# A hybrid HGRN2 / RWKV-7 layer on one core: level 0 from the forget gate, norms and sums in written order, output operands split behind the last in-projection column, one more step at sums and states

## The chip, the cores and the metric

The kernel runs on one core of one Trainium2 chip. The metric is the device time of one launch in microseconds, the median of three runs. The engines are named as in the profile: PE (TensorE, with PEld for its weight loads), DVE (VectorE), ACT (ScalarE), POOL (GpSimd, here mostly a queue that issues DMAs) and SP (SyncE, the other such queue).

## The reference

One decoder layer on x of 1 × 2048 × 1024, all in float32. In short (the recurrences are written out step by step; the kernel computes them by chunks of 64 tokens):

```python
h = _rmsnorm(x, norm1_w[l])
proj = h @ w_in[l]                       # 1024 -> 3840
hg_p, rw_p = proj[..., :HG_COLS], proj[..., HG_COLS:]

# HGRN2: 4 heads of 128
f = lb + (1.0 - lb) * sigmoid(f_raw)
q = silu(q_raw) * 128 ** -0.5
k = 1.0 - f
S = f_t * S + k_t v_t^T;  o_t = S^T q_t
o_hg = rms(o) * norm_w * silu(g_raw)

# RWKV-7: 8 heads of 64, token shift, low-rank decay / rate / gate
S = S * w_t + (S a_t) b_t^T + v_t k_t^T;  y_t = S r_t
o_rw = (groupnorm(y) * ln_w + ln_b + bonus) * g

x = x + concatenate([o_hg, o_rw], axis=-1) @ w_out[l]
x = x + _conv_ffn(_rmsnorm(x, norm2_w[l]), w_up[l], conv_w[l], conv_b[l], w_down[l])
```

and a final RMSNorm.

## The kernel before

The work falls into two phases. Phase 1, up to about 1314 us of the span, computes the in-projection, both recurrences, the output projection of three of the four token blocks and the second norm. Phase 2 computes the rest of the output projection and the ConvFFN with a Strassen-like split into seven products, for which sums of quarters of the operands are formed ahead (`four_sums`, L238). The diff touches phase 1 only.

Products of float32 operands are made of three matmuls on operands that are split into a high and a low part (`mm3`, L267 to L272): high × high, low × high, high × low. A split is a cast on ACT and a subtraction on DVE (`split_to`, L247 and L248, `split`, L254 and L255). All activations are issued through `act` (L122), which loads an activation table (L118) whenever the wanted function lies in another set than the last one.

Phase 1 interleaves three generators in program order:

- `dense` walks through a list of jobs. For each of the four blocks of 512 tokens there are 30 in-projection columns of 128 (job "P": eight k steps of three matmuls, each yielding 648 by its own count of ns). Columns are computed from the operands hh and hl, the split and normed x of the block, and are evicted from the PSUM banks `pj` (two of them) by `ev_q`, `ev_f`, `ev_v`, `ev_g`, `ev_rkv`, `ev_lora` and `ev_gd`. Among the columns stand extra jobs: loads of the next block's rows (`load4`), their norms (`norm4`, with `rstd`, L128, whose Square writes the tile nsq), the transposes into hh and hl ("T", `turn`, L443) and the transposes of the second norm ("N", L264). At the start of block 2 stands the output projection of block 0 ("O", `out_block`), at the start of block 3 that of block 1, and at the end that of block 2, whose operands are split by `o_take`.
- `rw_stream` runs eight `rw_super`, one for each block and half of the RWKV heads.
- `hg_stream` runs sixteen `hg_unit`, one for each block and HGRN2 head.

One turn of the main loop takes one step of `rw_stream`, one step of `hg_stream`, each up to its next `yield`, and then steps of `dense` until 2000 ns by its counts are used up (`TICK`, `fill`). So a `yield` more in a recurrence puts some 2000 ns of dense work by that count between the code ahead of it and the code behind it. Tile, the framework, then orders each engine's instructions: an instruction may move ahead of earlier written ones of its engine when its inputs are expected sooner. `tc.keep_in_program_order(i)` keeps an instruction behind all those that are written ahead of it on its engine. Data waits are made by semaphores.

The places that the change and the prediction name:

- L847: the matmuls of `rw_super` that multiply with the inverse; their results lie in the two banks `rw` and are copied by ACT into UV (x4) and M (x3). L867 is the first product behind it (tile xp, in one of the same two banks), L881 the products of M, with the additions L884 and L887 on DVE. L905 and L910 are the chain over the eight chunks, XH the state (L912).
- `hg_unit`: k = 1 − f (L947, tile hk, one buffer), the scaled operands hX of levels 0 to 6 (`scaled`, L971), the output product (L1064, L1065), the sum of squares (tile osq in hk's buffer, split into part, L1083 and L1084), the last products (L1076, L1077) and the store to oT.
- `out_block`: 32 weight tiles woraw (L395, loaded through POOL into the four buffers of the tag wraw, split at L254) and, for blocks 0 and 1, the operands oraw (L388, loaded through SP into two buffers of the tag sg and split into hh and hl during the first pass).

Of the kernel before, what the change touches and what calls it, by code (L numbers as in the profile page):

```python
# [7 lines left out]
F32 = mybir.dt.float32  # L8
# [59 lines left out]
def tile_layer(ctx, tc, consts, x, norm1_w, w_in, hg_lb_logits, hg_norm_w, rw_shift_mu, rw_w0, rw_w2,  # L68
# [56 lines left out]
            tab["uses"].append(i_)  # L125
        return i_

    def rstd(pool, xt, name, sqt="nsq", sqb=1):  # L128

        sq = pool.tile([P, D], BF16, tag=sqt, name="nsq", bufs=sqb)  # L130
        st = pool.tile([P, 2], F32, tag="nst", name=name, bufs=8)
        act(sq, xt, AF.Square, accum_out=st[:, 0:1])
        act(st[:, 1:2], st[:, 0:1], AF.Ln, bias=eps6, scale=1.0 / D)
        act(st[:, 1:2], st[:, 1:2], AF.Exp, scale=-0.5)
        return st[:, 1:2]
# [101 lines left out]

    def four_sums(b11, b12, b21, b22):  # L238

        V.tensor_sub(b11, b12, b11)  # L240
        V.tensor_sub(b12, b22, b12)
        V.tensor_sub(b22, b22, b11)
        V.tensor_sub(b21, b21, b22)
        return b11, b22, b12, b21
# [29 lines left out]
    def phase1(c1):  # L274
# [104 lines left out]
        def out_block(nb, oh=None, ol=None, then=None):  # L379


            for i2 in range(2):
                for dh in range(2):
                    accs = [bank("pj") for _ in range(2)]
                    for k in range(KD):
                        if i2 == 0 and dh == 0 and oh is None:
                            raw = stg("sg", "oraw", 2)
                            dma(raw, oT[nb][k * P:(k + 1) * P, :])  # L388
                            split_to(hh[:, k, :], hl[:, k, :], raw)
                        if i2 == 1 and dh == 0 and oh is not None:  # L390
                            raw = stg("sg", "oraw", 2)[:, 0:256]
                            dma(raw, oT[nb][k * P:(k + 1) * P, 256:512])
                            split_to(hh[:, k, 256:512], hl[:, k, 256:512], raw)
                        raw = wp.tile([P, 512], F32, tag="wraw", name="woraw", bufs=4)
                        wload(raw, w_out[0, k * P:(k + 1) * P, dh * 512:dh * 512 + 512])  # L395
                        wh, wl = split(wp, raw, [P, 512], "w", 4)
                        if k == KD - 2:
                            inputs = dh == 0 and (i2 == 0) == (oh is None)
                            xh = [wp.tile([P, BLK], F32, tag="wraw", name="xh", bufs=4) if inputs else
                                  stg("sg", "xh", 2) for _ in range(2)]  # L400
                            for q in range(2):
                                t0 = nb * BLK + (i2 * 2 + q) * P
                                dma(xh[q], x[0, t0:t0 + P, dh * 512:dh * 512 + 512])
                        for q in range(2):
                            is_ = slice((i2 * 2 + q) * P, (i2 * 2 + q + 1) * P)
                            lhs = ((hh[:, k, is_], hl[:, k, is_]) if oh is None or i2 == 1 else
                                   (oh[k // 4][:, k % 4, is_], ol[k // 4][:, k % 4, is_]))
                            mm3(accs[q], lhs, (wh, wl), k == 0, k == KD - 1)
                            if i2 == 1 and dh == 1 and q == 1:
                                next_block(then, k)  # L410
                            yield 680
                    for q in range(2):
                        V.tensor_add(xh[q], accs[q], xh[q])
                        r0 = (i2 * 2 + q) * P
                        (nc.gpsimd.dma_start if nb == NBLK - 2 and i2 and dh else dma)(
                            x1d[nb][r0:r0 + P, dh * 512:dh * 512 + 512], xh[q])
# [10 lines left out]
        def norm4(key):  # L427
            def f():
                for i in range(4):
                    t_ = rows[key][:, i, :]  # L430
                    V.tensor_scalar_mul(t_, t_, rstd(wp, t_, "nst", "wraw", 4))
            return f

        def four_tiles(t_):
# [12 lines left out]
        def split_h(nb, k):  # L447
# [3 lines left out]
            act(h4, src, AF.Copy, scale=w)  # L451
            V.scalar_tensor_tensor(l4, src, w, h4.bitcast(F32), ALU.mult, ALU.subtract)

        def next_block(nb, k):

            if nb is not None and nb < NBLK:
                for k_ in ([k - 2] if 2 <= k < KD - 1 else [k - 2, k - 1, k] if k == KD - 1 else []):
                    split_h(nb, k_)

        def sum_load(m):  # L460

# [12 lines left out]
        def o_take(m):  # L474

            def f():
                if m == 0:
                    t_ = xp_.tile([P, 2, 2, 4, 256], F32R, tag="xt", name="ohl", bufs=1)
                    rows["O"] = [[t_[:, c, i] for i in range(2)] for c in range(2)]
                t_ = wp.tile([P, 2, 256], F32, tag="wraw", name="oraw", bufs=4)  # L480
                dma(t_, oT[2][2 * m * P:2 * (m + 1) * P, 0:256].rearrange("(k p) t -> p k t", p=P))
                ks = slice(2 * (m % 2), 2 * (m % 2) + 2)
                split_to(rows["O"][0][m // 2][:, ks, :], rows["O"][1][m // 2][:, ks, :], t_)
            return f

        def to_h(k, tp, w):
# [29 lines left out]
        def dense():  # L516
# [64 lines left out]
            for n, jb in enumerate(jobs):  # L581
                if jb[0] == "E":
                    jb[1]()
                    continue
                if jb[0] == "A":
                    if jb[1] == 0:
                        banks = spread()
                        ahead = transposed(four_tiles(rows[0]), "n1", lambda: next(banks), to_h)
                    continue
                if jb[0] == "T":  # L590
                    yield from turn(jb[1])
                    continue
# [12 lines left out]
                while not cond():  # L605
                    yield None
                load(i)
                ws = loaded.pop(i)
                if i == 0:
                    next(ahead)  # L610
                    next(ahead)
                    constants()
                load(i + 1)
                i += 1
                acc = bank("pj")
                then = jobs[n + 1][1] if jobs[n + 1][0] == "A" else None
                for k in range(KD):
                    wh, wl = ws[k // 4]
                    next(ahead, None)
                    mm3(acc, (wh[:, k % 4, :], wl[:, k % 4, :]), (hh[:, k, :], hl[:, k, :]), k == 0, k == KD - 1)  # L620
                    if k == KD - 1:
                        ev(acc)
                        if fin is not None:
                            fin()
                    next_block(then, k)
                    yield 648

        def last_dma(nb):
# [18 lines left out]
        def rw_super(nb, s_):  # L647
# [208 lines left out]
            for e in range(2):  # L856
                r0, c0 = er0(e), col0(1, e)
                act(M[r0:r0 + 64, 0, 1, :, :, 0:64], quv[1][c0:c0 + 64, :, :, 0:64], AF.Copy)
            yield
            XH = tile_("XH", [2, 9, 64], "XH")  # L860
            V.tensor_copy(XH[:, :, 0, :], Xc[:, 2 * s_:2 * s_ + 2, :])
            xp = bank2()
# [81 lines left out]
        def hg_unit(nb, j):  # L944
# [15 lines left out]
            def scaled(l):  # L960
# [4 lines left out]
                V.tensor_mul(vw(X)[:, :, 1, :], vw(q)[:, :, 1, :], vw(Pf)[:, :, 1, :])  # L965
                n_ = BLK // (2 * m)
                if l == 0:
                    act(vw(X)[:, :, 0, :], vw(k)[:, :, 0, :], AF.Copy)
                    act(vw(Sf)[:, :, 0, :], vw(Pf)[:, :, 1, :], AF.Copy)
                else:  # L970
                    V.tensor_mul(vw(X)[:, :, 0, :], vw(k)[:, :, 0, :], vw(Sf)[:, :, 0, :])  # L971
                    V.tensor_mul(vw(Sf)[:, :, 0, :], vw(Sf)[:, :, 0, :],
                                 vw(Pf)[:, :, 1, m - 1:m].broadcast_to([P, n_, m]))
# [106 lines left out]
            yield  # L1080

# [543 lines left out]
```

## Time and profile before

| | us |
|---|---|
| runs | 2646.72, 2646.23, 2655.82 (median 2646.72) |
| the profiled execution: its time | 2645.42 |
| its span, first to last instruction | 2643.6 |
| PE busy over the span | 2547.0 (96%) |
| ACT busy over the span | 1372.7 (52%) |
| DVE busy over the span | 1963.7 (74%) |
| mean granted TensorE clock | 0.994 |

The profile is that of one execution. PE is busy for nearly the whole span, and the chain of waits lies for 70% on PE; a busy PE is not one at its peak, since matmuls are pipelined. What a change in phase 1 is worth is therefore read from PE's idle time there, from what ends it, and from the stretches with a lower granted clock.

### The profile page before, as it was taken

Reading aid. Unit: us, or ns where it says so; the run is one execution under the profiler, and the core shown is the slowest. Engines: PE = TensorE matmul, PEld = TensorE weight load, DVE = VectorE, ACT = ScalarE, POOL = GpSimd, SP = SyncE. Lnnn points to the kernel's source line nnn. Section 1 sums busy time; section 2 is a strip of 40 time slices with the busy share of each in tenths; the row PEclk is TensorE's granted clock in tenths of the full one; section 3 lists DMA queues with packets and bytes.
Section 4 is the critical chain, followed back from the end, with each engine's and each line's share of the span. In section 5 each row is a group of like instructions: output and inputs, shape, how many; then the busy total and the mean of one; then the engine's idle time right before and its main releaser. Section 6 shows DMA issues by size and latency. Waiting matters only on the chain.

```text
span 2643.6 us, 51054 instructions
## 1 busy us (share of the span) xinstructions
PE 2547.0 (96%) x19467; PEld 2046.8 (77%) x19467; DVE 1963.7 (74%) x3744; ACT 1372.7 (52%) x2258; POOL 382.1 (14%) x686
## 2 busy tenths in 40 slices
PE   7999999999999999899899999999999999999998
PEld 5877777777777767777678888887888887888887
DVE  4868677676576765777678789988988887766556
ACT  5555444555545555344466654556554544545444
POOL 6433222212222122232100000000000000000000
PEclk9999999999999999999999999999999999999999
DMA  8846463555655565845583467747763553998655
GB/s 304 239 147 195 152 168 116 143 159 205 190 173 138 174 212 179 261 151 150 181 287 124 136 221 257 240 154 232 245 203 129 171 171 128 334 321 283 200 191 187
DMA packets 380298, 518.98 MB, mean 196 GB/s; under 512 B 114463, under 2 KB 211093, under 8 KB 380053
## 3 DMA queue, kind: packets, MB, share of 16 engines
q1 hardware_dynamic: 325521, 337.38, 40.1%
q0 software_dynamic: 54464, 178.32, 20.9%
q8 instruction: 153, 2.51, 0.4%
q14 instruction: 92, 0.75, 0.1%
q10 hardware_dynamic: 68, 0.02, 0.0%
HBM read 372.99 MB, written 134.22 MB: 192 GB/s over the span
## 4 chain that ended last, share of the span: by engine, by line
PE 70%; DVE 11%; ACT 8%; DMA 7%; issue 3%; POOL 0%; SPq 0%; DVEq 0%; ACTq 0%; POOLq 0%
PE pj L270 7%; PE pj L271 7%; PE pj L272 6%; PE ua L270 5%; PE ua L272 5%; PE ua L271 5%; PE da L271 3%; PE da L272 3%; PE da L270 3%; PE ud L271 2%; PE ud L270 2%; PE ud L272 2%; PE db L272 2%; PE db L271 2%; PE db L270 2%
## 5 line engine op out<-in xcount | busy, mean ns | idle before, releaser
L270 PE MATMUL pj<-hh,wh 128*128 128x512 f32 x960 | 391.6, 408 | 6.1 <-ACT rkv L122 4.0
L271 PE MATMUL pj<-hl,wh 128*128 128x512 f32 x960 | 377.4, 393 | 0.0
L272 PE MATMUL pj<-hh,wl 128*128 128x512 f32 x960 | 377.4, 393 | 0.0
L270 PE MATMUL ua<-Bh,uwh 128*128 128x512 f32 x704 | 276.4, 393 | 3.5 <-ACT m L122 2.2
L272 PE MATMUL ua<-Bh,uwl 128*128 128x512 f32 x704 | 274.3, 390 | 0.0
L271 PE MATMUL ua<-Bl,uwh 128*128 128x512 f32 x704 | 274.1, 389 | 0.0
L270 PEld LDWEIGHTS pj<-hh,wh 128*128 128x128 f32 x960 | 180.9, 189 | 54.5 <-issue 7.0
L272 PEld LDWEIGHTS pj<-hh,wl 128*128 128x128 f32 x960 | 180.8, 188 | 39.4 <-DMA wl<-Win171l 0.3
L271 PEld LDWEIGHTS pj<-hl,wh 128*128 128x128 f32 x960 | 181.0, 189 | 35.0 <-DVE hl L488 0.5
L254 ACT CAST uwh<-uraw 128x512 fp32r<-128x512 f32 x220 | 134.3, 617 | 135.0 <-PE ua L271 55.7
L255 DVE TENSOR_TENSOR dal<-draw,dah 128x512 fp32r<-128x512 f32 x138 | 95.2, 690 | 108.3 <-ACT dah L254 105.7
L255 DVE TENSOR_TENSOR uwl<-uraw,uwh 128x512 fp32r<-128x512 f32 x220 | 147.1, 684 | 34.3 <-ACT uwh L254 34.3
L254 ACT CAST dah<-draw 128x512 fp32r<-128x512 f32 x138 | 85.8, 621 | 160.0 <-PE da L271 75.5
L270 PEld LDWEIGHTS ua<-Bh,uwh 128*128 128x128 f32 x704 | 132.2, 188 | 33.9 <-ACT m L122 5.6
L272 PEld LDWEIGHTS ua<-Bh,uwl 128*128 128x128 f32 x704 | 132.2, 188 | 28.1 <-DVE uwl L255 0.4
L271 PEld LDWEIGHTS ua<-Bl,uwh 128*128 128x128 f32 x704 | 132.3, 188 | 26.7
L270 PE MATMUL ud<-Bh,uwh 128*128 128x512 f32 x352 | 138.0, 392 | 0.0
L1495 POOL DMA_DIRECT2D gd<-y x2 | 1.1, 542 | 943.1 <-DVE y L1493 943.1
L272 PE MATMUL ud<-Bh,uwl 128*128 128x512 f32 x352 | 137.1, 390 | 0.0
L271 PE MATMUL ud<-Bl,uwh 128*128 128x512 f32 x352 | 137.0, 389 | 0.0
L271 PE MATMUL da<-dbl,dah 128*128 128x512 f32 x332 | 129.4, 390 | 0.2 <-DVE dbl L255 0.2
L272 PE MATMUL da<-dbh,dal 128*128 128x512 f32 x332 | 129.2, 389 | 0.0
(582 smaller groups left out, 6203.0 us busy)
## 6 DMA issues: line engine op xcount, KB each, us to landing
uraw<-in_w_up_dram SPq DMA_DIRECT2D x176, 256.0 KB, 3.2
woraw<-in_w_out_dram POOLq DMA_DIRECT2D x96, 256.0 KB, 3.6
br<-gd SPq DMA_DIRECT2D x88, 256.0 KB, 4.3
draw<-Sg SPq DMA_DIRECT2D x88, 256.0 KB, 3.0
draw<-Tw SPq DMA_DIRECT2D x88, 256.0 KB, 3.9
gd<-y SPq DMA_DIRECT2D x86, 256.0 KB, 3.0
Sg<-br SPq DMA_DIRECT2D x72, 256.0 KB, 2.2
xt<-x1d SPq DMA_DIRECT2D x32, 512.0 KB, 6.5
```

Of the source, the lines that this page charges most:

```text
L254: S.copy(hi, src)
L255: V.tensor_sub(lo, src, hi.bitcast(F32))
L270: TE.matmul(acc, lh, rh, start=first, stop=False, skip_group_check=skip)
L271: TE.matmul(acc, lh, rl, start=False, stop=False, skip_group_check=skip)
L272: TE.matmul(acc, ll, rh, start=False, stop=last, skip_group_check=skip)
L1495: (dma if end is None else nc.gpsimd.dma_start)(gd_[2 * h + b][fb * P:(fb + 1) * P, :], ys[0][:, b * BLK:(b + 1) * BLK])
```

## The change

It has seven parts. (1) The Square of the norms in `norm4` is kept in program order. (2) So is the first subtraction of `four_sums`, on which the other three depend. (3) The operands oraw of O 0 and O 1 are loaded and split by a new function `next_out` behind the k steps of the last in-projection column ahead of the block (operand k−2 behind step k), into buffers of the tag wraw, where the weights wraw and woraw lie too; that column now waits, in program order, until both recurrences of the output block are written. (4) `o_take`'s splits are kept in program order. (5) `rw_super` has one step more between the state copies (UV, M) and L867, and `hg_unit` one more between the split of the squares and L1083. (6) At level 0 the even half of hX is made on ACT from f, as 1 − f, instead of a copy of k. (7) The last product of `hg_unit` is written into gg (tile hgg) and stored from there, instead of from osq.

```diff
-    def rstd(pool, xt, name, sqt="nsq", sqb=1):
+    def rstd(pool, xt, name, sqt="nsq", sqb=1, pin=False):
...
-        act(sq, xt, AF.Square, accum_out=st[:, 0:1])
+        i_ = act(sq, xt, AF.Square, accum_out=st[:, 0:1])
+        if pin:
+            tc.keep_in_program_order(i_)
...
     def four_sums(b11, b12, b21, b22):
 
-        V.tensor_sub(b11, b12, b11)
+        tc.keep_in_program_order(V.tensor_sub(b11, b12, b11))
...
-                        if i2 == 0 and dh == 0 and oh is None:
-                            raw = stg("sg", "oraw", 2)
-                            dma(raw, oT[nb][k * P:(k + 1) * P, :])
-                            split_to(hh[:, k, :], hl[:, k, :], raw)
...
-                    V.tensor_scalar_mul(t_, t_, rstd(wp, t_, "nst", "wraw", 4))
+                    V.tensor_scalar_mul(t_, t_, rstd(wp, t_, "nst", "wraw", 4, pin=True))
...
+        def behind(k):
+
+            return [k - 2] if 2 <= k < KD - 1 else [k - 2, k - 1, k] if k == KD - 1 else []
...
+        def next_out(nb, k):
+
+            for k_ in behind(k):
+                raw = wp.tile([P, 512], F32, tag="wraw", name="oraw", bufs=4)
+                dma(raw, oT[nb][k_ * P:(k_ + 1) * P, :])
+                split_to(hh[:, k_, :], hl[:, k_, :], raw)
...
-                split_to(rows["O"][0][m // 2][:, ks, :], rows["O"][1][m // 2][:, ks, :], t_)
+                for i_ in split_to(rows["O"][0][m // 2][:, ks, :], rows["O"][1][m // 2][:, ks, :], t_):
+                    tc.keep_in_program_order(i_)
...
-                while not cond():
+                after = jobs[n + 1][1] if jobs[n + 1][0] == "O" and jobs[n + 1][1] < 2 else None
+                while not cond() or after is not None and (done["rw2"] < 2 * after + 2 or done["hg"] < 4 * after + 4):
                     yield None
...
                     next_block(then, k)
+                    if after is not None:
+                        next_out(after, k)
                     yield 648
...
                 act(M[r0:r0 + 64, 0, 1, :, :, 0:64], quv[1][c0:c0 + 64, :, :, 0:64], AF.Copy)
+            yield
             yield
             XH = tile_("XH", [2, 9, 64], "XH")
...
-                    act(vw(X)[:, :, 0, :], vw(k)[:, :, 0, :], AF.Copy)
+                    act(vw(X)[:, :, 0, :], vw(f)[:, :, 0, :], AF.Identity, bias=1.0, scale=-1.0)
...
             split_to(hi, lo, sq)
             yield
+            yield
             ms = bank("hg")
...
-            V.tensor_mul(sq, sq, gg)
-            last_dma(nb)(oT[nb][j * P:(j + 1) * P, :], sq)
+            V.tensor_mul(gg, sq, gg)
+            last_dma(nb)(oT[nb][j * P:(j + 1) * P, :], gg)
```

The change moves many instructions that it doesn't touch. The counts on PE, DVE, POOL and SP are the same before and after; ACT has twelve table loads more, all in phase 1. Three places, with the line numbers of each kernel's own code (the helpers of the changed one stand two lines lower):

ACT at the end of the first `rw_super`, before: ZT and TTs are copies of the inverse, rkv an eviction of a column, hX the copy at level 0 of the next `hg_unit`, UV and M the state copies, wh a cast of weights.

```order
L122 ACTIVATE TTs<-rw 32x8x32 x4
L122 ACTIVATE rkv_1763<-pj,omu 128x512
L254 CAST wh<-wraw 128x512
L122 ACTIVATE hX<-hk 128x256
L122 ACTIVATE UV<-rw 64x4x128 x4
L122 ACTIVATE M<-rw 128x8x64
L122 ACTIVATE M<-rw 64x8x64 x2
L122 ACTIVATE VT<-hg 128x512
```

The same place in the changed kernel:

```order
L122 ACTIVATE TTs<-rw 32x8x32 x4
L122 ACTIVATE rkv_1760<-pj,omu 128x512
L256 CAST wh<-wraw 128x512
L122 ACTIVATE UV<-rw 64x4x128 x4
L122 ACTIVATE M<-rw 128x8x64
L122 ACTIVATE M<-rw 64x8x64 x2
L122 ACTIVATE VT<-hg 128x512
```

The level-0 operation has left its place ahead of the state copies. On PE, 9 to 13 matmuls of dense columns stood between L847 and the product behind the state copies, and 12 to 20 stand there now; between the last output product of `hg_unit` and its sum of squares there were 6 to 12, and there are 9 to 36.

ACT at the start of block 2, before: the Squares nsq of the second norm of block 0 stand among the evictions of the first columns (tl and rkv).

```order
L122 ACTIVATE hh<-xt,vt 128x512 x2
L122 ACTIVATE nsq,nst<-xt 128x1024
L122 ACTIVATE tl<-pj,omu 128x512
L122 ACTIVATE nsq,nst<-xt 128x1024
L122 ACTIVATE tl<-tl 64x512
L122 ACTIVATE nsq,nst<-xt 128x1024 x2
L122 ACTIVATE rkv_7891<-pj,omu 128x512 x2
```

In the changed kernel they stand ten columns later, behind the eviction hf and ahead of hv, the eviction of the one column between the norm and its transposes:

```order
L122 ACTIVATE hf<-pj 128x512
L122 ACTIVATE nsq,nst<-xt 128x1024
L118 ACT_TABLE_LOAD
L122 ACTIVATE nst<-nst,eps_71 128x1
L122 ACTIVATE hX<-hf 128x256
L122 ACTIVATE nst<-nst 128x1
L122 ACTIVATE nsq,nst<-xt 128x1024
L122 ACTIVATE Sf<-hf 128x256
L122 ACTIVATE nst<-nst,eps_71 128x1
```

Behind these rows two more groups of Square, Ln and Exp follow, then a table load and hv. At the turns to the next block (the "T" jobs) hf stands ahead of the two Squares mk of `rw_super`, behind which it stood.

POOL's queue far ahead of O 0, before: Win are the split weights of later columns, woraw the first four of the 32 weight tiles of O 0.

```order
L575 DMA wl<-Win200l 128x512
L395 DMA woraw<-in_w_out_dram 128x512
L575 DMA wh<-Win201h 128x512
L575 DMA wl<-Win201l 128x512
L395 DMA woraw<-in_w_out_dram 128x512 x3
L575 DMA wh<-Win210h 128x512
```

The only place of O 0's weights on that queue in the changed kernel:

```order
L585 DMA wh<-Win281h 128x512
L585 DMA wl<-Win281l 128x512
L393 DMA woraw<-in_w_out_dram 128x512 x32
L585 DMA wh<-Win160h 128x512
L585 DMA wl<-Win160l 128x512
```

All 32 now follow each other behind the last column's weights; the first four take the buffers of the operands 4 to 7 of `next_out`. In both kernels the last recurrence matmul is followed by dense matmuls of the last output block: 24 before, 18 now.

More of the change, by code (lines that the diff above doesn't have):

```diff
@@ L452, in split_h @@
             V.scalar_tensor_tensor(l4, src, w, h4.bitcast(F32), ALU.mult, ALU.subtract)
+        def behind(k):
+            return [k - 2] if 2 <= k < KD - 1 else [k - 2, k - 1, k] if k == KD - 1 else []
         def next_block(nb, k):
             if nb is not None and nb < NBLK:
-                for k_ in ([k - 2] if 2 <= k < KD - 1 else [k - 2, k - 1, k] if k == KD - 1 else []):
+                for k_ in behind(k):
                     split_h(nb, k_)
+        def next_out(nb, k):
+            for k_ in behind(k):
+                raw = wp.tile([P, 512], F32, tag="wraw", name="oraw", bufs=4)
+                dma(raw, oT[nb][k_ * P:(k_ + 1) * P, :])
+                split_to(hh[:, k_, :], hl[:, k_, :], raw)
         def sum_load(m):
```

## Prediction

> **What bounds the kernel now.** I read the windows first, because the kernel has two phases and the change touches only the first. Columns: window, its length, then busy time and instructions of PE, PEld, DVE, ACT and POOL, the granted clock, the DMA share, GB/s.
>
> ```profile
> 20.00:1314.00 1294.00, 1229.20 (x13653) 963.61 (x13652) 900.71 (x2124) 654.35 (x1091) 354.27 (x633) 0.99 0.59 179
> 1314.00:2643.60 1329.60, 1313.24 (x5798) 1080.15 (x5798) 1055.29 (x1595) 706.53 (x1141) 15.01 (x28) 1.00 0.64 212
> ```
>
> PE is busy for 1229.2 of the 1294 us that the projections and recurrences take, and for 1313 of 1330 us behind them. Phase 2 keeps its instructions and their order, so I give it no change. The number of matmuls is the same as well. What can be won is PE's idle time in phase 1, about 65 us, and the time at half clock. Next, who ends that idle time (total, times, longest):
>
> ```profile
> PE rw L867 <- ACT M L122: 9.7, 6, 3.6
> PE pj L270 <- ACT hh L247: 6.0, 5, 2.0
> PE hg L1084 <- DVE part L248: 4.4, 7, 1.8
> PE rw L881 <- DVE AR L887: 4.3, 1, 4.3
> PE pj L443 <- ACT hf L122: 4.1, 2, 2.1
> PE pj L270 <- ACT rkv L122: 4.0, 2, 3.1
> PE rw L881 <- issue: 1.5, 1, 1.5
> PE hg L1083 <- ACT part L247: 1.1, 2, 1.0
> ```
>
> These eight rows are 35 us, and each has an edit aimed at it. The other idle time is in rows of under 4 us that no edit names.
>
> **The change part by part.** Sums are made against the profiled execution: 2645.42 us, a span of 2643.6 and 1.8 around it. The median of the runs is 2646.72, 1.3 more, which I add at the end.
>
> *States (one more step ahead of L867).* L867 needs the bank that the copies UV and M empty. The longest wait, in the chain of waits and on ACT:
>
> ```profile
> 144.40 4.51 DMA oT<-osq
> 148.91 0.02 issue
> 148.94 0.44 DVE hk L947
> ...
> 149.40 0.45 ACT L122 ACTIVATE hX<-hk 128x256 f32<-128x256 f32 x1 [3.65 <-DVE hk L947]
> 149.86 2.40 ACT L122 ACTIVATE UV<-rw 64x512 f32<-64x512 f32 x4
> 152.27 1.82 ACT L122 ACTIVATE M<-rw 128x512 f32<-128x512 f32 x3
> ```
>
> A store of 4.51 us holds the buffer hk; the copy hX<-hk waits for it, and the state copies wait behind hX on ACT. The level-0 and hgg edits take both out of ACT's order. The step does the rest: from the first UV to the end of the first M are 2.40 + 0.6 = 3.0 us. In the order of instructions 9 to 13 dense matmuls stood between L847 and L867, now 12 to 20, six of eight times 17 or more. One takes 0.24 us:
>
> ```profile
> 158.65 0.24 PE pj L271
> ```
>
> So the cover grows from 2.1–3.1 us to 4.0–4.8 us six times, and to 2.9 us twice. I take **−8.2** of the 9.7 (ends: 0 and −9.7). The level-0 and hgg edits beyond that: nothing, since the rest of ACT's wait on hk has no wait of PE behind it.
>
> *Sums (one more step ahead of L1083).* The square, its split and the subtraction are about 0.6 + 0.6 + 0.7 = 1.9 us (the cast below, as the nearest row, is 0.617). 6 to 12 dense matmuls covered them, 1.4 to 2.9 us; now 9 to 36 do, mostly over 15. **−4.5** of 5.5 (ends 0 and −5.5).
>
> *four_sums.* Two subtractions stood on DVE ahead of L887, waiting for loads:
>
> ```profile
> 1104.70 1.22 DVE L240 TENSOR_TENSOR xt<-xt 128x1024 f32<-128x1024 f32 x1 [3.96 <-DMA xt<-h2d]
> 1108.78 1.23 DVE L241 TENSOR_TENSOR xt<-xt 128x1024 f32<-128x1024 f32 x1 [2.25 <-DMA xt<-h2d]
> ```
>
> Pinned in written order, three columns behind their load, they find the data there. 4.3 + 1.5 goes: **−5.8** (ends +2, the 2.25 us met elsewhere on DVE, and −5.8).
>
> *Norms.* At the start of the fourth block the Squares stood ahead of an eviction that frees a pj bank:
>
> ```profile
> 979.07 1.06 ACT L122 ACTIVATE nsq<-xt 128x1024 bf16<-128x1024 f32 x1 [7.84 <-DMA xt<-x1d]
> ...
> 988.23 1.06 ACT L122 ACTIVATE nsq<-xt 128x1024 bf16<-128x1024 f32 x1 [1.31 <-DMA xt<-x1d]
> 989.19 0.19 ACT L122 ACTIVATION_READ_ACCUMULATOR nsq<-xt 128x1 f32 x1
> 989.28 1.25 ACT L122 ACTIVATE rkv<-pj,omu 128x512 f32<-128x512 f32 x2
> ```
>
> The pin puts them ten columns later; PE's 3.1 us behind rkv goes: **−3.5** (0 to −4.0). But they then stand one column ahead of the transposes that need them, twice (blocks 3 and 4). Behind hf (0.6) come a table load and four groups of Square, sum, Ln and Exp:
>
> ```profile
> L118 ACT ACT_TABLE_LOAD x44 | 56.5, 1283 | 1.5 <-PEq L1610 0.7
> L122 ACT ACTIVATE nst<-nst,eps 128x1 f32<-128x1 f32 x24 | 6.3, 284 | 0.1
> L122 ACT ACTIVATION_READ_ACCUMULATOR nsq<-xt 128x1 f32 x24 | 4.5, 188 | 0.0
> L122 ACT ACTIVATE nst<-nst 128x1 f32<-128x1 f32 x24 | 4.5, 191 | 0.1
> L431 DVE TENSOR_SCALAR xt<-xt,nst 128x1024 f32<-128x1024 f32 x20 | 14.2, 755 | 0.8 <-ACT nst L122 0.8
> ```
>
> That is 0.6 + 1.28 + 4 × (1.05 + 0.19 + 0.28 + 0.19) = 8.7, and 0.76 on DVE: 9.5 us. PE has one column there, 24 × 0.24 = 5.8 us, and recurrence matmuls. Idle is 1 to 4 us at each, behind xt on DVE: **+5** for both (0 to +9).
>
> *Turns.* PE waits 4.1 us because hf stood behind two Squares:
>
> ```profile
> 493.51 2.14 ACT L122 ACTIVATE mk<-mk 128x1024 f32<-128x1024 f32 x2
> 495.67 1.28 ACT L118 ACT_TABLE_LOAD   x1
> 496.96 0.60 ACT L122 ACTIVATE hf<-pj 128x512 f32<-128x512 f32 x1
> ```
>
> In the new order hf is ahead of them, 2.1 us earlier: **−3** (+2 to −4.1).
>
> *Output operands.* oraw's loads and casts leave the first pass of blocks O 0 and O 1, and 4.0 of the 6.0 us of the row L270 <- hh go (the other 2.0 is at O 2, the row below). But the raw tiles now lie in the four buffers of woraw. So the first four woraw, prefetched far ahead until now, are issued only when the last splits free those buffers; all 32 weight loads stand in one row on POOL's queue:
>
> ```profile
> 1277.86 0.79 PE L270 MATMUL pj<-wh,hh 128*128 128x512 f32 x1 [1.99 <-ACT hh L247]
> woraw<-in_w_out_dram POOLq DMA_DIRECT2D x96, 256.0 KB, 3.6
> L254 ACT CAST wh<-woraw 128x512 fp32r<-128x512 f32 x96 | 58.6, 617 | 79.2 <-PE pj L272 50.9 <-DMA woraw<-in_w_out_dram 11.4 <-DVE A L1016 5.0
> ```
>
> The chain from the last in-projection matmul to the first O matmul: oraw's cast and subtraction 0.6 + 0.7, load 3.6, cast and subtraction 1.3, with a sigmoid and a table load in between, 1.9: about 8 us. PE has the recurrences' matmuls for part of it. New idle is 2 to 7 us at each, I take 4, the middle, since the splits 4 and 5 come a step earlier: +8. Net **+4** (−4 to +14). Pinning o_take's splits I cost at nothing: two columns stand between them and O 2.
>
> *Table loads.* 12 more on ACT: 12 × 1.283 = 15.4 us. ACT is busy for 654 of 1294 us, and those at turns and norms are counted. For the rest **+2** (0 to +15.4).
> The Trainium skill (ScalarE: Activation LUTs, section "What ACT_TABLE_LOAD costs") has 2.66 us for a switch, the load and a drain of 1.38 us; by it ACT's term would be an estimated 31.9 us before cover. The trace differs: the load at 495.67 begins 0.02 us behind the Squares' end and hf 0.01 us behind its own.
>
> *Clock.*
>
> ```profile
> 143.00:160.00 17.00, 13.34 (x232) 10.81 (x235) 8.52 (x20) 8.37 (x16) 4.22 (x7) 0.90 0.38 126
> 562.00:575.00 13.00, 10.95 (x178) 7.38 (x180) 11.76 (x23) 8.23 (x18) 1.08 (x2) 0.87 0.67 197
> 1100.00:1120.00 20.00, 13.96 (x238) 10.87 (x232) 12.71 (x23) 5.78 (x11) 2.68 (x5) 0.83 0.69 250
> ```
>
> With the waits of L867 and L881 go 17 × 0.10 = 1.7 and 20 × 0.17 = 3.4: **−5.1** (0 to −6.8, with the 1.7 of 562 to 575).
> The Trainium skill (TensorE: Matmul & The Clock Gate, "HAM oscillation — how this bites in real kernels") lets only idle gaps of over about 3.4 us cost clock, which would leave my new waits free. The window from 562 does not agree: it ran at 0.87, and its wait was within the 2.0 us that the row of hh has as its longest. So each new wait of 2 to 4 us may cost another 1.7 us, four of them 6.8, which I put into the range.
>
> Sum: −8.2 − 4.5 − 5.8 − 3.5 − 3 − 5.1 = −30.1, and +5 + 4 + 2 = +11: **−19.1**, 2626.3 for the profiled execution, **2628** on the median.
>
> **Rivals.** *The waits only move.* The gains come, −30.1, but the norms' and the operands' waits at their upper ends, 9 + 14, with two clock dips, 3.4, and the table loads' 2: −1.7, **2645**. For it: the transposes and the output blocks each put a chain of 8 to 9.5 us against 6 us of dense work. Against it: the recurrences' matmuls stand there too.
>
> *Slower: the recurrences set the pace.* A turn gives dense 2 us by its own counts. 120 columns × 8 × 0.648, 192 output steps × 0.680 and 5 × 8 turn steps × 0.436 make 770 us, 385 turns of 1294 / 385 = 3.4 us. Eight supers take a step more each: 8 × 3.4 = 27 us if dense work has run out behind them, with the sixteen units' steps beside those of the supers. With half of the 30 won and the 11 of new waits: −15 + 11 + 27 = +23, **2670**. It decides from the point at which no dense matmul is left at phase 1's end. Against it: in the order 18 dense matmuls (24 before) still stand behind the last recurrence matmul, and the slip of 0.4 to 1.6 columns in the first blocks is made up at the third.
>
> *It doesn't do what it says.* If L867 still waits, behind evictions in place of hX, 8.2 + 1.7 come back: 2638.
>
> **How the numbers follow.** Forecast 0.57; waits move 0.22; L867 still waits 0.10; slower 0.11. About 0.5% (13 us) is what a measurement of this kernel can tell from no change: 2633.5 to 2660. The forecast's own spread puts some 0.04 over 2633.5 and the first rival's as much below it, and 0.01 of the first rival lies over 2660: faster 0.57, same 0.31, slower 0.12. The best bounds, −9.7 − 5.5 − 5.8 − 4.0 − 4.1 − 6.8 − 4, less the +0 ends, give −40: 2607. The upper end takes in both middle rivals and ten more, a third of the gain not coming: 2655. Left out are the slower rival and the tails, under 2 in 10.
>
> **What would show it.** Rows L867 <- M, L1084 <- part and L881 <- AR under 2 us each; no Square ahead of rkv at 979; idle of L264 behind xt at the N transposes, 1 to 4 us twice; L270 behind wh or woraw at the start of O 0 and O 1; 56 table loads in place of 44 in phase 1; phase 1 ending near 1295 instead of 1314 with phase 2 unchanged. The forecast is wrong if O's or N's new waits exceed 7 us, if the clock dips behind them, or if phase 1 ends with waits at L905 and L910 and no dense matmul beside them.

## The result: slightly slower, and the profile after

The changed kernel took 2659.94 us (median of 16 runs, 2652.95 to 2668.09), the kernel before 2651.24 us on the same chip (2645.53 to 2658.83); the ratio is 1.0037, 95% interval 1.0027 to 1.0047. A second series on another chip gave 1.0031 (1.0018 to 1.0044). So the change costs about 0.3%, 8 to 10 us, where 19 us of gain were forecast, and the time lies above the stated range.

The profiled execution took 2658.31 us, a span of 2656.4. The windows first; the second row is the passage to phase 2 (columns as before).

```profile
20.00:1314.00 1294.00, 1232.75 (x13644) 967.85 (x13643) 899.50 (x2116) 664.41 (x1095) 351.33 (x628) 0.98 0.58 179
1314.00:1327.00 13.00, 6.94 (x18) 4.25 (x17) 7.84 (x13) 6.53 (x11) 2.36 (x4) 0.64 0.79 245
1327.00:2656.40 1329.40, 1312.78 (x5789) 1079.63 (x5788) 1051.33 (x1589) 705.03 (x1137) 14.04 (x26) 1.00 0.64 209
```

Phase 2 takes as long as it did. Phase 1 and the passage take 13 us more. PE's idle time in them is 1294 − 1232.75 + 13 − 6.94 = 67 us, against 65 before: nothing was won there in sum. What grew is the time at a lower clock: 0.98 for 0.99 in the first row, 0.64 in the passage. The mean clock fell from 0.994 to 0.988; as lost time, span times (1 − clock), that is 2643.6 × 0.006 = 16 us before and 2656.4 × 0.012 = 32 us now. The difference is more than the whole loss, since this figure counts time at half clock as lost even where PE was idle in it: it is an upper bound. PE's busy time bears it out: with the same matmuls it grew by 1232.75 + 6.94 − 1229.20 = 10.5 us, its idle time by 2.5. So most of the 13 us are matmuls that took longer.

What ends PE's idle time now (total, times, longest):

```profile
PE pj L272 <- ACT wh L256: 6.5, 7, 4.1
PE pj L441 <- ACT hf L122: 4.5, 1, 4.5
PE rw L1098 <- ACT part L249: 4.4, 5, 2.5
PE pj L441 <- ACT xt L122: 3.8, 4, 1.7
PE wacc L1285 <- DVE Bl L250: 3.6, 1, 3.6
PE rw L895 <- DVE AR L901: 2.6, 2, 1.3
PE hg L1004 <- issue: 2.6, 3, 1.3
PE pj L272 <- ACT hh L249: 2.6, 1, 2.6
PE wacc L1285 <- ACT Bh L249: 2.1, 1, 2.1
PE pj L272 <- ACT xt L122: 1.7, 1, 1.7
PE rw L881 <- ACT M L122: 1.1, 2, 0.9
```

L881 is the old L867, L895 the old L881, L441 the old L443. The waits that the edits aimed at are mostly gone: 1.1 of 9.7 behind M, none behind rkv, none in `hg_unit`'s sums. As much came up elsewhere: weights of the output blocks (wh, 6.5), the turns (hf 4.5, xt 3.8), the first products of phase 2 (wacc, 5.7, which wait for their operands Bh and Bl).

The stretches around the dips of the clock:

```profile
210.00:240.00 30.00, 22.40 (x144) 18.07 (x143) 27.75 (x42) 20.50 (x29) 9.67 (x16) 0.83 0.54 147
568.00:590.00 22.00, 19.22 (x345) 13.82 (x347) 14.02 (x35) 10.37 (x21) 4.30 (x8) 0.84 0.44 144
820.00:850.00 30.00, 25.56 (x133) 19.34 (x132) 26.67 (x36) 23.83 (x33) 4.28 (x8) 0.89 0.40 118
893.00:907.00 14.00, 9.90 (x43) 8.45 (x44) 9.13 (x31) 5.19 (x9) 3.77 (x7) 0.76 0.60 184
1040.00:1060.00 20.00, 18.50 (x112) 13.81 (x111) 14.40 (x25) 12.59 (x26) 1.62 (x3) 0.74 0.40 136
1270.00:1290.00 20.00, 15.30 (x223) 11.65 (x222) 13.04 (x34) 7.67 (x19) 1.62 (x3) 0.83 0.64 201
1310.00:1332.00 22.00, 15.94 (x55) 11.51 (x54) 12.25 (x18) 11.16 (x17) 2.36 (x4) 0.77 0.67 212
```

Length times (1 − clock) is the loss of each: 5.1, 3.5, 3.3, 3.4, 5.2, 3.4 and 5.1 us, 29 us together: the first turn to a next block, the inverse of a `rw_super` beside O 0, the sums of one beside the third turn, O 1, the transposes of the second norm, O 2 and the passage.

The passage, in the chain of waits:

```profile
1309.39 1.24 DVE yo L939
...
1313.14 0.70 ACT osq L122
...
1316.92 0.71 POOL oT L953
1317.63 6.00 DMA oT<-hgg
...
1323.75 0.70 DVE Bl L250
...
1324.50 1.65 PE wacc L1285 x3
```

The last recurrences finish behind the last dense matmul: the last osq (L122, its Ln and Exp) ends on ACT at 1314.49, the last dense matmul of O 2 starts on PE at 1314.46. The operand Bl of phase 2's first products then waits for the store of 6.00 us. In the kernel before, the same place had

```profile
PE wacc L1270 <- DVE Bl L248: 1.1, 1, 1.1
```

### The profile page after: what moved, and what is told of

Read it like the earlier page. It is cut to its first block, busy times and chain, and to the rows that moved or that the text cites. A ratio compares the mean times of both kernels' runs of the same rounds, so it can differ in the third digit from the quotient of the medians.

```text
span 2656.4 us, 51081 instructions
## 1 busy us (share of the span) xinstructions
PE 2558.2 (96%) x19467; PEld 2055.6 (77%) x19467; DVE 1967.7 (74%) x3744; ACT 1389.2 (52%) x2270; POOL 381.9 (14%) x686
## 4 chain that ended last, share of the span: by engine, by line
PE 57%; DVE 6%; ACT 6%; DMA 5%; issue 4%; POOL 0%; SPq 0%; DVEq 0%; ACTq 0%; POOLq 0%
PE ua L272 5%; PE ua L273 5%; PE ua L274 5%; PE pj L272 4%; PE pj L273 3%; PE pj L274 3%; PE da L273 3%; PE da L274 3%; PE da L272 3%; PE ud L274 2%; PE ud L273 2%; PE ud L272 2%; PE db L272 2%; PE db L274 2%; PE db L273 2%
## 5 line engine op out<-in xcount | busy, mean ns | idle before, releaser
L273 PEld LDWEIGHTS ua<-Bl,uwh 128*128 128x128 f32 x704 | 132.2, 188 | 26.7
```

The costliest lines, as they stand in the source:

```text
L273: TE.matmul(acc, lh, rl, start=False, stop=False, skip_group_check=skip)
```

## The experiments

Two theories stood first: the extra steps lose (the slower rival), or the norms and the operands do. All ratios are against the kernel before on the same chip. The two columns behind are means over the runs: span × clock, the time that it would take at full clock, and span × (1 − clock), the time lost to it; the clock is given to three places, so each run's figure is good to 1.3 us. In brackets the kernel before on that chip. The last column is an upper bound for what the clock cost, as said above.

A warning for all that follows: c0 and the profile above are two executions of one kernel, and their dips differ. c0's has half clock at 138 and at 500 us (3.4 us each), where the first has none, and 13.7 us of it at the transposes instead of 10.2. So a single dip that comes or goes in one profile of an edit isn't shown to be the edit's doing; a wait of PE that repeats is firmer ground.

| run | edit | ratio, 95% interval | at full clock | lost |
|---|---|---|---|---|
| c0 | the changed kernel | 1.0031 [1.0018, 1.0044] | 2620.5 (2624.4) | 34.5 (21.8) |
| e1 | without both steps | 0.9985 [0.9972, 0.9999] | 2612.4 (2620.9) | 26.1 (21.6) |
| e2 | norms not pinned | 1.0021 [1.0006, 1.0036] | 2619.0 (2620.9) | 29.4 (21.6) |
| e3 | operands in the first pass | 1.0021 [1.0004, 1.0038] | 2619.3 (2620.9) | 29.7 (21.6) |
| e4 | no steps in the last units | 1.0005 [0.9989, 1.0020] | 2614.7 (2620.9) | 28.6 (21.6) |
| e5 | level 0 and store as before | 1.0037 [1.0021, 1.0054] | 2622.4 (2621.9) | 30.8 (20.9) |
| e6 | without the states step | 1.0005 [0.9991, 1.0019] | 2611.0 (2621.9) | 32.5 (20.9) |
| e7 | without the sums step | 0.9982 [0.9971, 0.9993] | 2612.5 (2621.9) | 26.7 (20.9) |
| e8 | e1 and e3 together | 0.9985 [0.9970, 1.0000] | 2615.0 (2621.9) | 23.5 (20.9) |
| e9 | before + level 0 and store | 0.9973 [0.9959, 0.9987] | 2621.2 (2624.4) | 17.5 (21.8) |
| e10 | before + four_sums' pin | 0.9976 [0.9965, 0.9988] | 2622.3 (2624.4) | 18.0 (21.8) |
| e11 | combined | 0.9935 [0.9918, 0.9953] | 2610.9 (2624.4) | 18.4 (21.8) |
| e12 | before + both steps | 1.0043 [1.0028, 1.0057] | 2626.4 (2621.0) | 27.4 (21.6) |
| e13 | combined + sums step but in the last unit | 0.9970 [0.9960, 0.9980] | 2611.6 (2621.0) | 22.6 (21.6) |

**e1, the changed kernel without both steps.**

```diff
             yield
-            yield
             XH = tile_("XH", [2, 9, 64], "XH")
...
             yield
-            yield
             ms = bank("hg")
```

> The changed kernel without the two extra steps (states, sums). Theory A, the steps cost more than they win (the end of phase 1 comes 4 to 5 us later, with 10.2 us at half clock behind it, and twelve table loads at the turns): the time falls by 5 to 15 us against the changed kernel, to 0.995 to 1.000 of the kernel before, and the 53 table loads of before come back. Theory B, the steps win (8.6 us of L867) and the loss is in the norms or the operands: the waits of L867 come back, 5 to 9 us, and the time rises by as much, to a ratio of 1.005 to 1.008.

The time fell by 0.46 to 0.52% against the changed kernel's two ratios, some 13 us, and ended below the kernel before. Theory A's numbers came, B's did not. The waits of `hg_unit`'s sums came back (5.8 us, 5.5 before the change), and the time fell all the same. PE's waits ahead of the product behind the state copies stayed low without the step:

```profile
PE rw L880 <- ACT M L122: 3.3, 8, 1.0
```

So of the 9.7 us only 2.2 (3.3 − 1.1) are the step's part here; the other edits take the rest (e9: those of level 0 and the store).

**e2, the norms' Squares not pinned.**

```diff
-                    V.tensor_scalar_mul(t_, t_, rstd(wp, t_, "nst", "wraw", 4, pin=True))
+                    V.tensor_scalar_mul(t_, t_, rstd(wp, t_, "nst", "wraw", 4))
```

> The changed kernel with the norms' Squares no longer kept in program order. Theory C, the pin costs at the transposes of the second norm: the half clock at 1048 (10.2 us long, 5.1 lost) and the 1.5 us of gaps there go, -5 to -7 us; the stall behind rkv at the start of block 3 may come back, +3 to +5. Under theory A alone: within 3 us of the changed kernel.

0.1 to 0.16% faster than the changed kernel, with intervals that overlap: not shown to differ. The profile has no dip at the transposes, but 3.69 us behind rkv, as before the change. The dip can't be put down to the pin: the profiles of e1, e3, e4 and e6, pinned like the changed kernel, have none there either. The row behind part in `rw_super`'s sums (L1098, 4.4 us in the changed kernel) is 2.4 here. So the pin trades one stall for others, and neither a gain nor a loss by it is shown.

**e3, the operands inside the first pass again.**

```diff
                     for k in range(KD):
+                        if i2 == 0 and dh == 0 and oh is None:
+                            raw = stg("sg", "oraw", 2)
+                            dma(raw, oT[nb][k * P:(k + 1) * P, :])
+                            split_to(hh[:, k, :], hl[:, k, :], raw)
...
-                while not cond() or after is not None and (done["rw2"] < 2 * after + 2 or done["hg"] < 4 * after + 4):
+                while not cond():
...
-                    if after is not None:
-                        next_out(after, k)
```

> The changed kernel with the operands of O 0 and O 1 loaded and split inside the first pass again. Theory D, the first woraw wait for the splits' buffers: the 4.1 us of L270 behind wh at O 1 and the half clock there (6.8 us long, 3.4 lost) go, and the 6.8 at 577 too if it hangs on them: -7 to -11 us, with 2 to 4 us of waits behind hh in their place. Under theory A alone: within 3 us of the changed kernel.

The wait of 4.1 us at O 1 went (1.21 behind hh stands there) and the dips at 577 and 898 are not in this profile, but one of 6.8 us at 498 is, which the first profile of the changed kernel lacks. The ratio gives 3 to 4 us, half of what was expected and within the intervals' overlap. With e8, where the same edit wins nothing on top of e1, the operands' split is a small loss at most.

**e4, no extra step in the last rw_super and the last hg_unit.**

```diff
+            if 2 * nb + s_ < 2 * NBLK - 1:
+                yield
             yield
-            yield
             XH = tile_("XH", [2, 9, 64], "XH")
...
+            if 4 * nb + j < 4 * NBLK - 1:
+                yield
             yield
-            yield
             ms = bank("hg")
```

> The changed kernel with the extra steps left out in the last rw_super and the last hg_unit only. If the later end of phase 1 comes from the steps of the last two (4.7 us of idle at the first weights of phase 2 and 10.2 us at half clock there): -5 to -10 us. If the last store is late for another reason: within 3 us of the changed kernel, the gaps ahead of wacc staying at 3 us or more.

1.0005 against 1.0031 and 1.0037: 7 to 8.5 us are won by leaving out two steps of twenty-four. The window of the passage in this kernel:

```profile
1309.00:1322.00 13.00, 12.99 (x58) 10.28 (x57) 8.61 (x14) 4.42 (x8) 1.08 (x2) 1.00 0.94 327
```

PE has hardly any idle time in it and a full clock, where the changed kernel's passage had 6.94 of 13 us busy at 0.64.

**e5, level 0 from k and the store from osq again.**

```diff
-                    act(vw(X)[:, :, 0, :], vw(f)[:, :, 0, :], AF.Identity, bias=1.0, scale=-1.0)
+                    act(vw(X)[:, :, 0, :], vw(k)[:, :, 0, :], AF.Copy)
...
-            V.tensor_mul(gg, sq, gg)
-            last_dma(nb)(oT[nb][j * P:(j + 1) * P, :], gg)
+            V.tensor_mul(sq, sq, gg)
+            last_dma(nb)(oT[nb][j * P:(j + 1) * P, :], sq)
```

> The changed kernel with level 0 made from k again and the last product stored from osq again. If the level-0 and store edits, and not the step, took the wait ahead of the product behind the state copies (9.7 us before, 3.3 without the steps, 1.1 with them): some 2 to 5 us of that wait come back even with the step, ACT's idle behind hk returns to about 20 us, and the time is 0 to 6 us above the changed kernel. If the step alone covers it: the wait stays under 2 us.

The step covers the wait behind M too: the row of L881 behind M shows 0.8 us, and the time is that of the changed kernel. But a product further on now waits for AR, a row that the changed kernel's list of waits doesn't have:

```profile
PE rw L909 <- DVE AR L901: 7.7, 5, 4.1
```

Why is not shown. The step and the level-0 edits are two cures for one wait, and either of them takes most of it (for the steps in the kernel before, see e12).

**e6 and e7, one step each taken out.** The edits are the two halves of e1's.

> The changed kernel without the states step, the sums step kept. Without both steps the time was 14 us lower. If the steps cost by how far they push the recurrences' work back, the states step (8 of them) and the sums step (16) each carry a part: -3 to -8 us here. If only the sums step costs (it is on the last hg_unit's way to the last store): within 3 us of the changed kernel, with the gaps ahead of wacc staying.

> The changed kernel without the sums step, the states step kept. If the sums step carries the loss: -8 to -14 us, the gaps ahead of wacc (5.8 us) and the half clock there gone, fewer table loads than 65, and the waits of L1083 and L1084 in hg_unit (5.5 us before) back in part. If the states step carries it: within 4 us of the changed kernel.

Without the states step 1.0005, without the sums step 0.9982. Each undone wins by itself, 7 to 8.5 us and 13 to 15; both together win 13: they don't add, and the sums step carries more of it. The gaps ahead of wacc shrank without either: to 0.6 us without the states step, to 2.6 without the sums step. So at the end of phase 1 the sums step does little harm by itself. Without the sums step the waits of `hg_unit`'s sums came back in part, 2.9 us. Table loads in the program are 65 in the changed kernel, 63 without the states step, 59 without the sums step, 53 without both.

**e8, e1 and e3 together.**

> The changed kernel without both steps and with the operands of O 0 and O 1 split inside the first pass; what is left is the two kinds of pins, level 0 from f and the store from gg. If the costs add: 4 us below the kernel without steps alone, about 0.997 of the kernel before, faster than both. If the operands' loss hung on the steps (later recurrences, so later oT): the same as without the steps, 0.998 to 0.999.

0.9985, the same as e1.

**c0, the changed kernel once more.**

> The changed kernel once more, beside the others on one chip, so that span and granted clock of its runs stand beside those of the kernel before there. If the loss is clock: span times (1 - clock) is 12 to 15 us more than before on the mean of the runs, and span times clock, the time at full clock, is within 3 us of before. If the loss is waiting: the second figure is up by 8 us or more and the first by under 4.

Lost to the clock 34.5 us against 21.8; at full clock 2620.5 against 2624.4. By this split the change is about 4 us faster at full clock, and the clock turns it into a loss of 8 us. The split is rough, since the time at half clock holds idle time of PE; what stands is that the time at half clock grew and PE's idle time hardly did.

**e9, the kernel before with the level-0 and store edits alone** (the edits of e5, the other way).

> The kernel before with level 0 from f and the store from gg alone. If these edits took most of the wait behind the state copies (9.7 us, 3.3 in the changed kernel without steps): that wait falls to 3 to 5 us and the half clock at 153 goes, the time falls by 5 to 8 us, ratio 0.997 to 0.998. If it needs the step: under 2 us.

0.9973, with

```profile
PE rw L867 <- ACT M L122: 2.8, 6, 1.1
PE rw L881 <- DVE AR L887: 6.7, 1, 6.7
```

so 6.9 of the 9.7 us went, and the profile has no dip at 153. The wait behind AR is 6.7 us, 0.9 more than the 5.8 before.

**e10, the kernel before with four_sums' pin alone.**

```diff
-        V.tensor_sub(b11, b12, b11)
+        tc.keep_in_program_order(V.tensor_sub(b11, b12, b11))
```

> The kernel before with the pin on four_sums' first subtraction alone. If the term of the forecast was right: the 5.8 us ahead of L881 at 1108 and 1115 and the half clock there (6.8 long, 3.4 lost) go: -5 to -9 us, ratio 0.9965 to 0.998. If the wait moves to another place on DVE's order: under 3 us.

0.9976. The wait behind AR is down to 3.4 us, not gone, and the dip there to 3.4 us from 6.8; the clock lost 18.0 us instead of 21.8.

**e12, the kernel before with both steps alone** (e1's edit, the other way).

> The kernel before with both extra steps alone. If the steps are a loss by themselves (later last store, colliding turns, twelve table loads, all of which they bring here too): +2 to +12 us although up to 15 us of waits ahead of L867, L1083 and L1084 go; ratio 1.001 to 1.005, gaps ahead of wacc of over 4 us, half clock at the turn near 217 and at the end of phase 1. If they lose only together with the other edits: -5 to -12 us, ratio 0.9955 to 0.998.

1.0043: the steps are a loss by themselves, as large as that of the whole change, and its profile has the stall and the half clock of the changed kernel at the first turn (4.54 us behind hf). The gaps ahead of wacc were expected over 4 us and are 2.7. Of the wait behind M the steps by themselves take 5.7 of 9.7 us:

```profile
PE rw L868 <- ACT M L122: 4.0, 4, 2.2
```

**e11, combined, and e13, the same with the sums step put back except in the last unit.** e11 is the changed kernel with

```diff
-                              (at[nb] + 10, ("E", norm4(("N", nb - 2)))), (at[nb] + 11, ("N", nb - 2))]
+                              (at[nb] + 9, ("E", norm4(("N", nb - 2)))), (at[nb] + 11, ("N", nb - 2))]
...
+            if 2 * nb + s_ < 2 * NBLK - 1:
+                yield
             yield
-            yield
             XH = tile_("XH", [2, 9, 64], "XH")
...
             yield
-            yield
             ms = bank("hg")
```

> The changed kernel without the sums step, with the states step left out in the last rw_super, and with the second norm's Squares one column earlier (two columns ahead of their transposes). If the single costs add: 2 to 6 us below the kernel without the sums step alone, ratio 0.996 to 0.9975, no half clock at the transposes near 1048 and no gap of over 2 us ahead of wacc. If the clock's dips only move: about 0.998.

For e13 the sums step stands in `hg_unit` under the condition of e4.

> The combined kernel with the sums step put back, but not in the last hg_unit. If the sums step costs only at the end of phase 1: within 3 us of the combined kernel, ratio 0.9925 to 0.995. If it costs in the middle too (table loads, the turn near 217, 4.5 us behind hf): 5 to 10 us above it, ratio 0.9955 to 0.998.

e11 is faster than both kernels, 2630.47 us against 2648.98 on its chip, 0.9935, which is below the range that was expected if the single costs add. Its profile has no dip at the transposes or in the passage. e11 differs from e7 by two edits, the norms one column earlier and the last `rw_super`; they were not run apart. e13 stands at 0.9970: against the kernel before on each chip, the sums step costs another 9 us in the middle of phase 1. The two profiled executions don't show that difference (2632.76 us for e11, 2632.60 for e13); one place where the step costs is seen in them, the first turn. ACT in the changed kernel:

```profile
205.81 1.28 ACT L118 ACT_TABLE_LOAD   x1
207.11 0.69 ACT L122 ACTIVATE osq<-hg,eps 128x512 f32<-128x512 f32 x1
...
208.85 1.28 ACT L118 ACT_TABLE_LOAD   x1
210.15 0.60 ACT L122 ACTIVATE sgm<-pj 128x512 f32<-128x512 f32 x1
...
211.46 1.28 ACT L118 ACT_TABLE_LOAD   x1
212.75 1.06 ACT L122 ACTIVATE W<-mk 128x1024 f32<-128x1024 f32 x1
213.72 1.04 ACT L122 ACTIVATE ai<-mk 128x1024 f32<-128x1024 f32 x1
214.78 1.28 ACT L118 ACT_TABLE_LOAD   x1
216.07 0.60 ACT L122 ACTIVATE hf<-pj 128x512 f32<-128x512 f32 x1
```

and PE there, in the changed kernel:

```profile
216.72 1.11 PE L441 MATMUL pj<-ident,xt 128*128 128x128 f32 x4 [4.54 <-ACT hf L122]
219.58 1.11 PE L441 MATMUL pj<-ident,xt 128*128 128x128 f32 x4 [1.74 <-ACT xt L122]
```

One step later, the sum's Ln and Exp (osq) fall between the sigmoids of the next `rw_super` (ai) and of the column (sgm), so two more table loads stand ahead of the eviction hf that frees the bank for the turn. In e11 osq is through earlier, and PE waits 2.41 us there instead of 4.54; in e13 it is 4.54 again. The half clock there lasts 6.8 us in e11 and 10.2 in e13, but also 6.8 in c0 with its wait of 4.5. So 2.1 of the 9 us are located, and the rest is not.

## Why the prediction was wrong, by its own steps

- *States, −8.2.* The size was right, 9.7 to 1.1, the cause half right: e9 shows that the level-0 and store edits, costed at nothing beyond the step, take 6.9 us alone, e5 and e12 that the step does much the same (8.9 and 5.7). Beside them the step is worth 2.2 us, and it was not charged for what it pushes back. **This is the step that failed**: the extra steps' price in the recurrences was left to a rival at 0.11, "decides from the point at which no dense matmul is left". The forecast had the two steps and their table loads at −8.2 − 4.5 + 2 = −10.7 us. The runs have them at some +13 (e1, taken out of the changed kernel) and +11 (e12, put into the kernel before): some 24 of the 28 us between the forecast and the result.
- *The slower rival* had the direction and partly the mechanism. Its test, 18 dense matmuls left behind the last recurrence matmul, was the wrong one. Not the matmul but the last store decides: behind the last recurrence matmul come additions on DVE and ACT, 0.7 us of POOL and 6.00 us of DMA, together longer than 18 × 0.24 = 4.3 us of dense work. In e4 this end is worth 7 to 8.5 us. The rival's sum of +23 was too much by more than half.
- *Sums, −4.5.* The wait went (no row of `hg_unit`'s L1098 or L1099 is left), but the step cost more than it gave: e7 is 13 to 15 us faster without it. The row behind part in `rw_super` rose from 1.7 to 4.4 us, but not by the step: e1 has 4.4 without it, and e2, without the norms' pin, 2.4.
- *Table loads, +2.* There are 56 in phase 1 for 44 before, as the order had it, and at the first turn they stand on PE's path. Of what they cost, the runs show only the 2.1 us there (e11 against e13).
- *four_sums, −5.8.* Right in kind; 2.6 us remain behind AR in the changed kernel and 3.4 in e10, so 2.4 to 3.2 of the 5.8 went. With the clock the pin alone is worth some 6 us, ratio 0.9976.
- *Norms, −3.5 and +5.* The stall behind rkv went. At the transposes only 1.4 us of idle came (behind xt; the 0.7 behind hv were 0.6 before), but 5.2 us of clock in this profile. e2 shows that without the pin the old stall is back. Whether the dip at the transposes hangs on the pin or on the column between them is open: of the kernels with the norms where the changed kernel has them, c0, e5, e7 and e8 show it and e1, e3, e4 and e6 don't; e11, with one column more, doesn't either.
- *Turns, −3.* Wrong in sign: hf 4.1 to 4.5, xt 1.2 to 3.8 and a further 1.7. It was read from the second turn, where no row behind hf is left; at the first the sums step brought table loads.
- *Output operands, +4.* The first woraw wait came as described, 4.1 us at O 1, hardly at O 0; with 3.4 of hh won the net is +2.4. As a part of the loss it is not shown beyond the noise (e3).
- *Clock, −5.1.* The two dips named went, but the seven stretches above lose 29 us, where the whole span before lost 16. Over the whole span it is +13 us on the mean of c0's runs, +16 in the profile, idle time at half clock counted in. Of the terms this was the one missed by most, and it is no second loss beside the steps' price: without the steps it is 4.5 us instead of 12.7 (e1). The forecast put at most 6.8 us of it into the range.

The rule of the Trainium skill (TensorE: Matmul & The Clock Gate, section "What's actually happening") that a free-running window of about 3.4 us is watched fits the trace: the dips are 3.4, 6.8 or 10.2 us long (13.7 in c0) and within a profile begin on one grid. That an idle window is needed (the same section) the trace does not bear out: in phase 1 of both profiles no window ahead of a dip was idle. Four such windows of the changed kernel; a dip followed behind the first three, none behind the last:

```profile
833.00:836.40 3.40, 0.86 (x6) 0.54 (x4) 3.07 (x4) 3.40 (x5) 1.07 (x2) 1.00 0.85 281
894.40:897.80 3.40, 0.28 (x3) 0.09 (x1) 2.44 (x7) 1.21 (x2) 1.10 (x3) 1.00 0.83 258
1044.60:1048.00 3.40, 2.21 (x16) 1.52 (x16) 3.19 (x6) 3.31 (x7) 0.86 (x2) 1.00 0.45 154
495.10:498.50 3.40, 1.72 (x13) 1.17 (x12) 3.37 (x6) 3.39 (x5) 0.00 (x0) 1.00 0.02 5
```

In both profiles a window of this grid with PE busy for under 0.38 of it always had a dip behind it, and between 0.41 and 0.77 it went either way. It is not a rule for all runs: in e13 a window at 16 us, with PE busy for 0.17 of it, had none. Why PE busy for 2.21 of 3.4 us brings a dip and 1.72 none stays open; both windows hold 128 × 128 transposes, the first also small products of the recurrence.

Of the sums step's 9 us in the middle about half is the clock by the table's split: against the kernel before on its chip, e13 loses 1.0 us more to it and e11 3.4 less. The two ran on two chips, so this is rough.

Open is what holds the other edits back. The level-0 and store edits alone win 7 us (e9), the pin of `four_sums` alone 6 (e10), and e1, which has both and the remaining edits, only 4. Either the two don't add, or the norms' pin or that of `o_take`'s splits costs some 9 us beside them. The operands' split doesn't (e8); the pins were not taken out of a kernel without the steps.

## What to carry to other kernels

A step more between a producer and its consumer hides a wait only if nothing else hides it already, and everything behind it in its chain comes later. At the end of the chain, where the last store has no other work behind it, that is paid in full: leave the step out there, and look at the store, not at the last matmul. Ask of each moved step which activation functions now alternate on ACT, and whether an eviction that PE waits for stands behind the table loads. A wait can have a stretch at half clock behind it, and that can cost more than the wait; profile a kernel twice before putting one such stretch down to an edit.

## What was not expected of the hardware

The time at half clock changed by more than the balance of all waits that the change removed and added: 34.5 us of some 2657 are lost to it in the changed kernel, 21.8 before, 17.5 in the best of the single edits (idle time at half clock counted in), while PE's idle time in phase 1 and the passage grew by 2.5 us. It also differs between runs of the same kernel, from 26 to 37 us over the runs of c0, and with it much of the scatter of the times (2650.93 to 2662.01): their standard deviation is 3.8 us, and 2.0 at full clock.

Three dips of the changed kernel last 10.2 us: at the first turn, in the passage and at the second norm's transposes. In the first two PE is partly idle in the first two windows of the dip. At the transposes no wait was over 0.54 us, and PE was busy in every window of the dip, yet the half clock went on:

```profile
1047.70:1051.10 3.40, 3.40 (x14) 2.42 (x14) 1.66 (x3) 1.75 (x3) 0.00 (x0) 0.55 0.41 154
1051.10:1054.50 3.40, 3.40 (x14) 2.29 (x13) 1.97 (x5) 1.38 (x2) 0.00 (x0) 0.50 0.49 164
```

These windows mix 128 × 128 transposes with products of 64 rows. In the other dips of phase 1 of both profiles, one window with PE busy throughout ended the half clock, also one of transposes alone (third turn) and one of small products alone (the dip at 153 of the kernel before). What counts as busy there stays open.
